# The last product of a transformer block: where sums of activations stand, and how k-tiles are dealt out between quads

## The chip, the cores and the metric

One core of a Trainium2 chip runs the whole kernel. Its engines work side by side: TensorE multiplies matrices (PE in the profile, with its weight loads as PEld), VectorE (DVE) and ScalarE (ACT) do elementwise work, GpSimd (POOL) fills constants and issues a few transfers, and SyncE (SP) issues the transfers of the weights. The metric is the device time of one execution in microseconds, lower is better.

## The reference, cut to what matters

The kernel computes one block with a mixer and a feed-forward part, for 256 tokens and a width of 2048. The change touches the feed-forward part:

```python
h = rms_norm(x, norm_ffn_pre[l])
u = causal_depthwise_conv(h @ w_up[l], ffn_conv_w[l], ffn_conv_b[l])
u_g, u_v = jnp.split(u, 2, axis=-1)
x = x + rms_norm((jax.nn.silu(u_g) * u_v) @ w_down[l], norm_ffn_post[l])
```

`w_up` is 2048 x 11264 and `w_down` is 5632 x 2048, all in float32. The activations `silu(u_g) * u_v` (called a here) have 5632 features, which are 44 k-tiles of 128 features for the last product.

## The kernel before, in words

**Numbers in two parts.** Every float32 operand of a product is split into a high part (a copy to a shorter format, by ACT: `high`) and a low part (the difference, by DVE: `rest`). A product is three matmuls: high by high, high by low and low by high. A tile of weights of 128 x 1024 costs one ACT copy and one DVE subtraction.

**The up projection** (the loop at line 1173). For each of 44 k-tiles i two feature tiles of `w_up` are multiplied on TensorE (`ftile`, lines 151 to 183); DVE and ACT then scale them, apply the convolution of width three, and multiply the gate by the value. The result is split and stored in `gh` and `gl`. The temporary `a` comes from a ring of five buffers with the tag `fa`. The order of this work is left to a planner that simulates the engines and takes what has the highest priority; only some pieces carry a higher priority.

**The last product** (from line 1221). It is computed in two halves of 1024 output columns, `Pair(0)` and `Pair(1)`, each with four result banks (two token halves by two blocks of 512 columns). Of the 44 k-tiles, 28 are *plain* (list `PLAIN`): each costs 4 x 3 = 12 matmuls of 128 x 512. The other 16 are taken two at a time, in 8 pairs (`EARLY + LATE`): a *quad* treats two k-tiles by two token halves by two column blocks as a product of 2 x 2 blocks, and computes it with seven block products in place of eight, as Strassen and Winograd do. A quad so costs 7 x 3 = 21 matmuls instead of 24, but needs sums of weights and sums of activations.

The sums of weights are formed when a quad is prepared (`quad`, line 1267): four DVE additions of 512 columns between four pairs of `high` and `rest`, called b, a, t and 4 in the names of tiles (`whiq_7t` is the high part of t of quad 7).

The sums of activations (`sums`, line 1161) take a0 and a1 of the pair. For the pairs in `EARLY` they are formed in the up projection, as soon as the second k-tile is there, and kept in `se`. For the pairs in `LATE` they are formed in the last product by `late` (line 1329): DVE adds the two parts of both k-tiles back together, then five more DVE operations and two ACT copies follow; the results go to `sl`.

**What sets the order in the last product.** `fixed` (line 975) puts each instruction of DVE behind the one given before it, and the same for ACT, so that the order in the text is the order on these engines. `in_line` does the same for TensorE. The split weights live in a ring of four buffers for the high and four for the low parts (`ring`); a copy into a buffer waits until TensorE has finished with what was there. The raw weights arrive through SP's queue in a ring of five buffers (`fetch`, line 101); a fetch waits until its buffer is free. In the first half the program goes through the quads j = 0 to 7: some plain tiles, then the quad, then, for even j, the sums of `LATE` pair j // 2. The three remaining plain tiles come last. The second half has its own order, which also prepares six plain tiles ahead of time (`kept`).

**Other places that the change touches.** `diag` (line 291) writes a diagonal matrix that a small product spreads over the partitions; it is called for the first norm (names with h) and for the norm ahead of the feed-forward part (names with f). `ones2` is the constant operand of that second product. POOL's own transfers keep their descriptors in a space on chip whose size line 1501 gives.

Of the kernel before, what the change touches and what calls it, by code (L numbers as in the profile page):

```python
# [23 lines left out]
F32 = mybir.dt.float32  # L24
# [7 lines left out]
T = 256  # L32
# [2 lines left out]
NFT = FF // 128  # L35
EPS = 1e-6

EARLY = [(0, 1), (2, 3), (4, 5), (6, 7)]
LATE = [(8, 9), (11, 12), (13, 14), (15, 16)]
PLAIN = [*range(22, 33), 10, *range(17, 22), *range(33, NFT)]  # L40
BA, BB, BC, BG = 2100, 2200, 2200, 2500
PR = 1000
# [13 lines left out]
def block(ctx: ExitStack, tc: tile.TileContext, x, xf, fp, cst, rows, sgw, w1, w2, wf_a, wt_bv, wf_bu, wf_c,  # L56
          wt_vs, wf_q, wt_g, wt_p, wt_o, wf_up, wt_dn, wt_dq, out):
    nc = tc.nc
# [3 lines left out]
    P0 = ctx.enter_context(tc.tile_pool(name="p0", bufs=1))  # L62
# [88 lines left out]
    def ftile(src, mov):  # L151

        hs = granule(src)
        ps = PS.tile([128, 2, T], F32, tag="acc", name=f"ps{uid[0]}")
        mm_f(ps, hs, mov)
        return ps
# [54 lines left out]
    def fsum(ps, dst, scale=1.0, rb=None):  # L211

        t1 = T1["pool"].tile([128, T], F32, tag="q", bufs=T1["bufs"], name=f"t1_{uid[0]}")
        with tc.high_priority(offset=int(PR)):
            S.activation(t1, ps[:, 1], AF.Copy)  # L215
            V.tensor_add(t1 if rb is not None else dst, ps[:, 0], t1)  # L216
            if rb is not None:
                V.scalar_tensor_tensor(dst, t1, scale, rb, op0=ALU.mult, op1=ALU.mult)
# [28 lines left out]
    def q1(name, shape=(128, T)):  # L247
        return P1.tile(list(shape), F32, tag="q", bufs=12, name=name)
# [40 lines left out]
    G.memset(ones, 1.0 / 1024)  # L289

    def diag(r, nm):
        dg = P0.tile([128, 128], F32, tag="dg", bufs=2, name=f"dg{nm}")
        return dg, V.tensor_scalar(dg, ident, r, None, op0=ALU.mult).ins

    def norm1(parts, nm, n=1):

        v = PZ.tile([128, n], F32, tag=f"ssv{n}", bufs=4, name="ssv" + nm)
        V.reduce_sum(v, parts, axis=AX.X)
        variance[0] = V.tensor_scalar(v, v, 1.0 / D, EPS, op0=ALU.mult, op1=ALU.add).ins
        return rsqrt(PZ, v, n, nm)  # L300
# [55 lines left out]
    def rms_sum():  # L356

        ssp = bank([128, 2], "ssp")
        for t in range(2):
            in_line(lambda: PE.matmul(ssp[:, t:t + 1], lhsT=sq[:, 0, t * 128:t * 128 + 128], rhs=ones[:, 0:1],  # L360
                                      start=True, stop=True).ins)
        with tc.high_priority(offset=int(PR)):
            v = PZ.tile([128, 2], F32, tag="ssv2", bufs=4, name="ssvx")
            V.tensor_scalar(v, ssp, 1024.0 / D, EPS, op0=ALU.mult, op1=ALU.add)
            r0 = rsqrt(PZ, v, 2, "x")
            V.tensor_scalar(rh, r0, 0.5, None, op0=ALU.mult)
            return r0, [diag(r0[:, t:t + 1], f"h{t}")[0] for t in range(2)]
# [607 lines left out]
    def fixed(eng, op, *args, **kw):  # L975

        with ExitStack() as order:
            order.enter_context(tc.high_priority())
            for ins in seq.get(eng, ()):
                order.enter_context(tc.issue_after(ins))  # L980
            seq[eng] = [op(*args, **kw).ins]  # L981
# [131 lines left out]
    P2b_ctx = ExitStack()  # L1113
    se = P2.tile([128, 2, len(EARLY), 3, 128], R, name="se")
    gh = [P2.tile([128, 11, T], R, tag="gh", bufs=4, name=f"gh{i}") for i in range(4)]
    gl = [P2.tile([128, 11, T], R, tag="gl", bufs=4, name=f"gl{i}") for i in range(4)]
    P2b = P2b_ctx.enter_context(tc.tile_pool(name="p2b", bufs=1))
    T1["pool"], T1["bufs"] = P2b, 2
    rb2 = P2b.tile([128, T], F32, name="rb2")
    ones2 = P2b.tile([128, 128], F32, name="ones2")  # L1120
    G.memset(ones2, 1.0)
    raw = [fetch(wf_up[2][:, a:a + 1024], 1024) for a in (0, 1024)]
    hs = []
# [5 lines left out]
    with ExitStack() as order:  # L1129
        order.enter_context(tc.high_priority())  # L1130
        for ins in seq[V] + seq[S]:
            order.enter_context(tc.issue_after(ins))
        junk3 = P2b.tile([128, 512], mybir.dt.bfloat16, tag="fa", bufs=5, name="junk3")
        for t in range(2):
            for c in range(4):
                xc = y1[:, t, c * 512:c * 512 + 512]
                if c % 2:
                    V.scalar_tensor_tensor(junk3, xc, 1.0, xc, op0=ALU.mult, op1=ALU.mult,
                                           accum_out=ss2[:, t, c:c + 1])
                else:  # L1140
                    S.activation(junk, xc, AF.Square, accum_out=ss2[:, t, c:c + 1])
        r2 = norm1(ss2, "f", 2)
# [11 lines left out]
    def g2(k, ts):  # L1154

        return gh[k // 11][:, k % 11, ts], gl[k // 11][:, k % 11, ts]
# [4 lines left out]
    def sums(st, a0, a1, k0, dst, do=loose):  # L1161

        h, l = g2(k0, H2)
        do(V, V.tensor_add, st[:, 1], a0[:, H2], a1[:, H2])
        do(V, V.tensor_sub, st[:, 2], st[:, 1], a0[:, H1])
        do(V, V.tensor_sub, st[:, 3], a1[:, H1], st[:, 2])
        do(S, S.activation, dst[0], st[:, 1:4], AF.Copy)
        do(V, V.tensor_sub, st[:, 0], a0[:, H1], a0[:, H2])
        do(S, S.activation, h, st[:, 0], AF.Copy)
        do(V, V.tensor_sub, dst[1], st[:, 1:4], dst[0].bitcast(F32))  # L1170
        do(V, V.tensor_sub, l, st[:, 0], h.bitcast(F32))

    for i in range(NFT):
        acc = []
        for v in range(2):
            f = 2 * i + v
            with tc.issue_after(pe_last[0]):
                pu = pu2[f] if f < 3 else ftile(wf_up[f], h2)
            s = P2b.tile([128, T], F32, tag="fs", bufs=2, name=f"fs{f}")
            fsum(pu, s, rb=rb2)  # L1180
            a = P2b.tile([128, T], F32, tag="fa", bufs=5, name=f"fa{f}")
            w = [fps[:, C_FW + f * 3 + k:C_FW + f * 3 + k + 1] for k in range(3)]
            S.activation(a, s, AF.Identity, bias=fps[:, C_FB + f:C_FB + f + 1], scale=w[2])
            V.scalar_tensor_tensor(a[:, 1:T], s[:, 0:T - 1], w[1], a[:, 1:T], op0=ALU.mult, op1=ALU.add)
            V.scalar_tensor_tensor(a[:, 2:T], s[:, 0:T - 2], w[0], a[:, 2:T], op0=ALU.mult, op1=ALU.add)  # L1185
            acc.append(a)
        S.activation(acc[0], acc[0], AF.Silu)  # L1187
        V.tensor_mul(acc[0], acc[0], acc[1])
        ts = H1 if i in [k for k, _ in EARLY] else slice(0, T)
        h, l = g2(i, ts)  # L1190
        S.activation(h, acc[0][:, ts], AF.Copy)
        V.tensor_sub(l, acc[0][:, ts], h.bitcast(F32))
        for j, (k0, k1) in enumerate(EARLY):
            if i == k0:
                first = acc[0]
            elif i == k1:
                st = P2b.tile([128, 4, 128], F32, tag="st", name=f"st{j}")
                sums(st, first, acc[0], k0, (se[:, 0, j], se[:, 1, j]))
# [8 lines left out]
    gain = fin[:, 4096:5120]  # L1207
    sl = P2c.tile([128, 2, len(LATE), 3, 128], R, name="sl")
    turn = [0]

    def scratch():
        turn[0] ^= 1
        return fin[:, 5120 + 1024 * turn[0]:6144 + 1024 * turn[0]]

    PAIRS = EARLY + LATE
    ss3 = PZ.tile([128, 2, 8], F32, name="ss3")
# [9 lines left out]
    def rest(lo, x, hi):  # L1226
        fixed(V, V.tensor_sub, lo, x, hi.bitcast(F32))
# [11 lines left out]
    class Pair:  # L1239
# [27 lines left out]
        def quad(self, j):  # L1267
# [19 lines left out]
            rest(l4[:, L], b[:, U], h4[:, L])  # L1287
            src, n = (se, j) if j < len(EARLY) else (sl, j - len(EARLY))
            s1, s2, s4 = ((src[:, 0, n, i], src[:, 1, n, i]) for i in range(3))
# [39 lines left out]
    def late(j):  # L1329
        k0, k1 = LATE[j]  # L1330
        tmp = scratch()
        a = tmp[:, 0:512].rearrange("p (k t) -> p k t", k=2)
        gi, gk = divmod(k0, 11)
        fixed(V, V.tensor_add, a, gh[gi][:, gk:gk + 2].bitcast(F32), gl[gi][:, gk:gk + 2].bitcast(F32))
        sums(tmp[:, 512:].rearrange("p (s t) -> p s t", s=4), a[:, 0], a[:, 1], k0, (sl[:, 0, j], sl[:, 1, j]), fixed)

    NP, NQ, KEEP = len(PLAIN), len(PAIRS), 6
# [2 lines left out]
    first, second = Pair(0), None  # L1340
    i = 0
    for j in range(NQ):
        while i < (j + 1) * (NP - 3) // NQ + (j < 2):
            first.plain(i)
            i += 1
        first.quad(j)
        if j % 2 == 0:
            late(j // 2)
    for i in range(i, NP):
        first.plain(i)  # L1350
    first.combine()
# [2 lines left out]
    i = 0  # L1354
# [45 lines left out]
def _layout(inp):  # L1400
# [65 lines left out]
    plain = c(dn[:, PLAIN].transpose(0, 1, 3, 2, 4)).reshape(2, len(PLAIN), 128, 1024)  # L1466
    k0, k1 = [k for k, _ in EARLY + LATE], [k for _, k in EARLY + LATE]
    quads = np.concatenate([dn[:, k1, 1], dn[:, k1, 0], dn[:, k0, 0], dn[:, k0, 1]], axis=3)
# [42 lines left out]
```

## Time and profile before

| | |
|---|---|
| median of 3 runs | 1584.49 us (1583.78 to 1584.77) |
| profiled execution | 1583.9 us, with a span of 1582.2 us in the profile |
| PE busy | 1567.0 us, 99% of the span |
| DVE busy | 1215.6 us, 77% |
| ACT busy | 884.5 us, 56% |
| transfers | 303.75 MB, mean 192 GB/s |

The span is what the profiler records from the first to the last instruction; the time of the execution also has a little around it. Busy time of an engine is time in which an instruction is on it; the busy time of TensorE is modelled, so that the number of matmuls in a stretch says more than its busy share. In a row of the profile, L981 is line 981 of the kernel: all instructions that go through `fixed` carry that line, and are told apart by their tiles. `wraw`, `whi` and `wlo` are raw, high and low weights; `pd0` and `pd1` are the result banks of the two halves; `fin` is one large buffer that holds results and scratch.

### The profile page before, as it was taken

To read this page: it belongs to the slowest core of one execution; us is meant where nothing else is said; L and a number is where in the kernel's file an instruction comes from. 1 tells how busy PE (TensorE), PEld (TensorE's weight loads), DVE (VectorE), ACT (ScalarE), POOL (GpSimd) and SP (SyncE) were. 2 spreads that over 40 slices of the span, in tenths; PEclk is the share of its full clock that TensorE was granted. 3 is DMA by queue.
4 is the path that set the end of the run, shared out by engine and by line. 5 is a ranking of instruction groups with operands and counts; after the bars stand their busy time and mean duration, and the time that the engine had idled before them with its cause. 6 is when DMAs were issued, how large, how long until landed. Compare 5 with 4: busy or idle time off the path is not lost.

```text
span 1582.2 us, 22327 instructions
## 1 busy us (share of the span) xinstructions
PE 1567.0 (99%) x8185; PEld 1329.6 (84%) x8185; DVE 1215.6 (77%) x2082; ACT 884.5 (56%) x1430; POOL 17.8 (1%) x46
## 2 busy tenths in 40 slices
PE   9999999999999999999999999999999999999997
PEld 7888889888888787788888888888888888777886
DVE  7899999857865555465558987777777777888887
ACT  7544454447647675654456655555555555555563
POOL 1000020000000000000000000000000000000000
PEclk9999999999999999999999999999999999999999
DMA  9555556655764444565773665555555566566663
GB/s 370 187 193 180 191 174 212 195 190 186 236 197 157 156 144 156 162 198 188 241 235 117 198 190 190 188 192 189 188 187 188 190 190 202 168 200 207 211 229 106
DMA packets 84863, 303.75 MB, mean 192 GB/s; under 512 B 9744, under 2 KB 10768, under 8 KB 84240
## 3 DMA queue, kind: packets, MB, share of 16 engines
q1 hardware_dynamic: 83664, 298.11, 57.9%
q0 software_dynamic: 944, 4.19, 0.8%
q8 instruction: 64, 1.05, 0.3%
q14 instruction: 47, 0.39, 0.1%
q10 hardware_dynamic: 144, 0.02, 0.0%
HBM read 299.13 MB, written 2.10 MB: 190 GB/s over the span
## 4 chain that ended last, share of the span: by engine, by line
PE 98%; DVE 1%; ACT 0%; DMA 0%; issue 0%; SPq 0%; DVEq 0%; ACTq 0%
PE ps L173 29%; PE ps L180 15%; PE pd1a L1255 6%; PE pd0b L1255 6%; PE pg L194 6%; PE pg L193 6%; PE pg L195 6%; PE py L194 3%; PE py L195 3%; PE py L193 3%; PE po L193 2%; PE po L194 2%; PE po L195 2%; PE pd1b L1255 1%; PE pd0a L1255 1%; PE pv L193 1%
## 5 line engine op out<-in xcount | busy, mean ns | idle before, releaser
L145 DVE TENSOR_TENSOR wlo<-wraw,whi 128x1024 fp32r<-128x1024 f32 x440 | 536.2, 1221 | 171.8 <-ACT whi L144 164.8
L144 ACT ACTIVATE whi<-wraw 128x1024 fp32r<-128x1024 f32 x440 | 461.2, 1053 | 244.1 <-PE pg L195 100.9
L173 PE MATMUL ps<-h2T,whi 128*128 128x512 f32 x1360 | 325.0, 391 | 0.0
L173 PEld LDWEIGHTS ps<-h2T,whi 128*128 128x128 f32 x1360 | 249.8, 188 | 48.2
L180 PEld LDWEIGHTS ps<-h2T,wlo 128*128 128x128 f32 x1360 | 174.5, 191 | 6.7
L180 PE MATMUL ps<-h2T,wlo 128*128 128x256 f32 x1360 | 176.6, 283 | 0.0
L173 PE MATMUL ps<-hT,whi 128*128 128x512 f32 x640 | 157.4, 392 | 0.0
L215 ACT ACTIVATE t<-ps 128x256 f32<-128x256 f32 x125 | 47.6, 382 | 188.4 <-PE ps L173 188.2
L195 PE MATMUL pg<-whi,hT 128*128 128x512 f32 x384 | 150.9, 393 | 0.0
L194 PE MATMUL pg<-wlo,hT 128*128 128x512 f32 x384 | 150.7, 392 | 0.0
L193 PE MATMUL pg<-whi,hT 128*128 128x512 f32 x384 | 147.6, 393 | 0.0
L173 PEld LDWEIGHTS ps<-hT,whi 128*128 128x128 f32 x640 | 116.0, 188 | 21.3
L216 DVE TENSOR_TENSOR t<-ps,t 128x256 f32<-128x256 f32 x125 | 52.9, 424 | 80.3 <-ACT t L215 80.0
L476 DVE SCALAR_TENSOR_TENSOR cv<-hb,fps,cv 128x256 f32<-128x256 f32 x240 | 105.8, 485 | 0.2 <-ACT cv L472 0.2
L180 PEld LDWEIGHTS ps<-hT,wlo 128*128 128x128 f32 x640 | 84.7, 190 | 4.7
L180 PE MATMUL ps<-hT,wlo 128*128 128x256 f32 x640 | 86.8, 283 | 0.0
L194 PEld LDWEIGHTS pg<-wlo,hT 128*128 128x128 f32 x384 | 72.1, 188 | 16.2 <-issue 1.1
L195 PEld LDWEIGHTS pg<-whi,hT 128*128 128x128 f32 x384 | 72.1, 188 | 15.1 <-issue 0.7
L193 PEld LDWEIGHTS pg<-whi,hT 128*128 128x128 f32 x384 | 71.8, 188 | 14.8 <-issue 0.3
L981 DVE TENSOR_TENSOR wlowraw<-wraw,whiwraw 128x1024 fp32r<-128x1024 f32 x52 | 62.1, 1222 | 13.3 <-ACT whiwraw L981 12.3
L981 ACT ACTIVATE whiwraw<-wraw 128x1024 fp32r<-128x1024 f32 x52 | 53.8, 1055 | 16.6 <-PE ps L173 4.3
L1187 ACT ACTIVATE fa<-fa 128x256 f32<-128x256 f32 x44 | 18.3, 416 | 64.3 <-DVE fa L1185 64.3
(891 smaller groups left out, 2458.6 us busy)
## 6 DMA issues: line engine op xcount, KB each, us to landing
wraw<-in_wf_up_dram SPq DMA_DIRECT2D x176, 512.0 KB, 4.3
wraw<-in_wt_g_dram SPq DMA_DIRECT2D x96, 512.0 KB, 4.2
wraw<-in_wt_dn_dram SPq DMA_DIRECT2D x56, 512.0 KB, 4.6
wraw<-in_wt_p_dram SPq DMA_DIRECT2D x48, 512.0 KB, 4.1
wraw<-in_wf_a_dram SPq DMA_DIRECT2D x32, 512.0 KB, 3.9
wraw<-in_wt_o_dram SPq DMA_DIRECT2D x32, 512.0 KB, 4.6
wraw<-in_wt_dq_dram SPq DMA_DIRECT2D x32, 512.0 KB, 3.6
wraw<-in_wf_bu_dram SPq DMA_DIRECT2D x16, 512.0 KB, 4.4
```

The lines of the kernel that those rows point to most:

```text
L144: S.activation(hi[:, :n], raw[:, :n], AF.Copy)
L145: V.tensor_sub(lo[:, :n], raw[:, :n], hi[:, :n].bitcast(F32))
L173: ins = PE.matmul(ps[:, :, ts], lhsT=ws[k // 8][0][:, c:c + 128], rhs=mov[:, k, :, ts], start=(k == 0 and not t), stop=(k == n - 1), skip_ ...
L180: ins = PE.matmul(ps[:, 1, ts], lhsT=ws[k // 8][1][:, c:c + 128], rhs=mov[:, k, 0, ts], start=False, stop=False, skip_group_check=True).ins
L193: PE.matmul(ps, lhsT=xh, rhs=hi, start=first, stop=False)
L194: PE.matmul(ps, lhsT=xh, rhs=lo, start=False, stop=False)
L195: return PE.matmul(ps, lhsT=xl, rhs=hi, start=False, stop=last).ins
L215: S.activation(t1, ps[:, 1], AF.Copy)
L216: V.tensor_add(t1 if rb is not None else dst, ps[:, 0], t1)
L476: V.scalar_tensor_tensor(ca[:, j], hb[:, j, k:k + T], w(j, k), ca[:, j], op0=ALU.mult, op1=ALU.add)
L981: seq[eng] = [op(*args, **kw).ins]
L1255: ins = PE.matmul(bank, lhsT=a[x], rhs=w[y], start=first and j == 0, stop=last and j == 2).ins
```

## The change

The pair (8, 9) moves from `LATE` to `EARLY`, so that its sums of activations are formed in the up projection. The three sets of sums that stay in the last product are formed ahead of quads 1, 2 and 3, behind the plain tiles that stand before these quads, and no longer behind quads 0, 2, 4 and 6. The plain tiles of the first half are dealt out as 5, 4, 4, 4, 2, 2, 2, 2 ahead of the eight quads (before: 4, 3, 2, 3, 3, 3, 3, 4), with three left for the end as before. The order of the second half is as it was. To hold the larger `se`, memory is found elsewhere: the diagonal tiles and `ones2` take buffers of rings that exist already (`q` and `fa`), and the space for POOL's descriptors is halved.

```diff
-EARLY = [(0, 1), (2, 3), (4, 5), (6, 7)]
-LATE = [(8, 9), (11, 12), (13, 14), (15, 16)]
+EARLY = [(0, 1), (2, 3), (4, 5), (6, 7), (8, 9)]
+LATE = [(11, 12), (13, 14), (15, 16)]
...
     def diag(r, nm):
-        dg = P0.tile([128, 128], F32, tag="dg", bufs=2, name=f"dg{nm}")
+        dg = q1(f"dg{nm}", (128, 128)) if nm[0] == "h" else small(f"dg{nm}", (128, 128))
...
-    ones2 = P2b.tile([128, 128], F32, name="ones2")
+
+    def small(name, shape=(128, T), dt=F32):
+        return P2b.tile(list(shape), dt, tag="fa", bufs=5, name=name)
+
+    ones2 = small("ones2", (128, 128))
...
-        junk3 = P2b.tile([128, 512], mybir.dt.bfloat16, tag="fa", bufs=5, name="junk3")
+        junk3 = small("junk3", (128, 512), mybir.dt.bfloat16)
...
-            a = P2b.tile([128, T], F32, tag="fa", bufs=5, name=f"fa{f}")
+            a = small(f"fa{f}")
...
     for j in range(NQ):
-        while i < (j + 1) * (NP - 3) // NQ + (j < 2):
+        while i < (5, 9, 13, 17, 19, 21, 23, 25)[j]:
             first.plain(i)
             i += 1
+        if 1 <= j <= len(LATE):
+            late(j - 1)
         first.quad(j)
-        if j % 2 == 0:
-            late(j // 2)
...
-    nc = bacc.Bacc("TRN2", target_bir_lowering=False, num_devices=1, dynamic_dma_scratch_size=4096)
+    nc = bacc.Bacc("TRN2", target_bir_lowering=False, num_devices=1, dynamic_dma_scratch_size=2048)
```

## The prediction, made before the changed kernel ran

> **What bounds the kernel now.** I read the page first, then the clock and busy time in stretches, then the chain of waits and the order of time of each engine in the last product. The page says that TensorE sets the time:
>
> ```profile
> span 1582.2 us, 22327 instructions
> PE 1567.0 (99%) x8185; PEld 1329.6 (84%) x8185; DVE 1215.6 (77%) x2082; ACT 884.5 (56%) x1430; POOL 17.8 (1%) x46
> ```
>
> So only a place where TensorE runs below its own pace can give time back. The view by stretches (us from:to and length, then busy time and instruction count of PE, PEld, DVE, ACT, POOL, then the granted clock, DMA share, GB/s) finds it. The first two rows are the up projection with and without sums of pairs; the last two are the two column halves of the last product, `Pair(0)` and `Pair(1)`:
>
> ```profile
> 870.35:981.60 111.25, 111.25 (x644) 98.40 (x643) 96.92 (x181) 69.60 (x117) 0.00 (x0) 1.00 0.60 191
> 981.60:1092.90 111.30, 111.30 (x642) 98.35 (x641) 87.89 (x141) 63.81 (x100) 0.00 (x0) 1.00 0.59 190
> 1338.94:1458.90 119.96, 116.70 (x506) 94.44 (x505) 101.35 (x132) 63.16 (x73) 0.00 (x0) 1.00 0.60 193
> 1458.90:1573.16 114.26, 114.24 (x505) 94.25 (x503) 96.70 (x117) 62.77 (x76) 0.00 (x0) 1.00 0.57 189
> ```
>
> Both halves issue 28 x 12 + 8 x 21 = 504 matmuls of 128x512 (the rows count one or two of a neighbour), at the same clock of 1.00. The second takes 114.26 us, 0.2267 us for each; the first takes 119.96. The first half therefore holds 119.96 - 114.26 = 5.70 us in which TensorE waits. That is the whole stake of the change; nothing else in the span is slower than its own pace by more than parts of a us.
>
> TensorE's rows in order of time show where it waits (start, duration, instruction, in brackets the idle time and what ended it):
>
> ```profile
> 1354.36 0.39 PE L1255 MATMUL pd0b<-whiq,gl 128*128 128x512 f32 x1
> 1354.87 0.51 PE L1255 MATMUL pd0b<-whiwraw,gh 128*128 128x512 f32 x1
> 1356.12 0.51 PE L1255 MATMUL pd0b<-wlowraw,gh 128*128 128x512 f32 x1 [0.76 <-DVE wlowraw L981]
> 1356.47 0.40 PE L1255 MATMUL pd0b<-whiwraw,gl 128*128 128x512 f32 x1
> ```
>
> The quad's last matmul starts at 1354.36. At the pace the third matmul after it would start at 1354.36 + 3 x 0.227 = 1355.04; it starts at 1356.47, 1.43 late. The waits of this stage, added up (total us, times, longest), have four of this kind:
>
> ```profile
> PE pd0b L1255 <- DVE wlowraw L981: 3.0, 4, 0.8
> ```
>
> In order of time the four stand behind quads 0, 2, 4 and 6: exactly those after which `late` is called. (The bracket counts only the idle time; each wait also stretches the matmuls beside it, so the starts are the better measure.) 5.70 / 4 = 1.43 agrees with the wait worked out above, so these four are all of it.
>
> What made the weights late is seen on ACT and DVE:
>
> ```profile
> 1350.08 0.63 ACT L981 ACTIVATE whiq<-wraw 128x512 fp32r<-128x512 f32 x1 [1.27 <-PE pd0b L1255]
> 1353.13 0.52 ACT L981 ACTIVATE sl<-fin 128x384 fp32r<-128x384 f32 x1 [2.42 <-DVE fin L981]
> 1353.57 0.30 ACT L981 ACTIVATE gh<-fin 128x128 fp32r<-128x128 f32 x1
> 1353.77 2.94 ACT L981 ACTIVATE whiwraw<-wraw 128x1024 fp32r<-128x1024 f32 x3
> ```
>
> ```profile
> 1351.36 0.68 DVE L981 TENSOR_TENSOR fin<-gh,gl 128x512 f32<-128x512 f32 x1
> 1352.07 1.15 DVE L981 TENSOR_TENSOR fin<-fin 128x128 f32<-128x128 f32 x4
> 1353.69 0.56 DVE L981 TENSOR_TENSOR sl<-fin,sl 128x384 fp32r<-128x384 f32 x1 [0.47 <-ACT sl L981]
> 1354.17 0.28 DVE L981 TENSOR_TENSOR gl<-fin,gh 128x128 fp32r<-128x128 f32 x1
> 1354.85 3.50 DVE L981 TENSOR_TENSOR wlowraw<-wraw,whiwraw 128x1024 fp32r<-128x1024 f32 x3 [0.39 <-ACT whiwraw L981]
> ```
>
> The order on both engines is written out (`fixed`), and the buffers of split weights are a ring of four. The quad's last copy (`whiq`) waits for TensorE to free a buffer and so starts just when TensorE begins the quad. From there to the quad's end are only 21 x 0.227 = 4.76 us, and the sums take 3.49 of them (1351.36 to 1354.85). The next plain tile's copy stands behind the sums in ACT's line.
>
> **The change, part by part.**
>
> *Matmuls.* Same eight pairs, same plain tiles, same 504 matmuls for each half: 0.
>
> *Sums no longer behind a quad: -5.6.* After a quad without sums the next plain tile is in time. Behind quad 3:
>
> ```profile
> 1390.32 1.06 ACT L981 ACTIVATE whiwraw<-wraw 128x1024 fp32r<-128x1024 f32 x1 [0.73 <-PE pd0b L1255]
> 1391.42 3.90 DVE L981 TENSOR_TENSOR wlowraw<-wraw,whiwraw 128x1024 fp32r<-128x1024 f32 x3 [1.10 <-ACT whiwraw L981]
> 1393.70 0.39 PE L1255 MATMUL pd0b<-wlowraw,gh 128*128 128x512 f32 x1
> ```
>
> One third of the 3.90 is 1.30, so the low part is ready at 1392.72 and needed at 1393.70: 0.98 to spare. With the change every quad is followed this way. The first wait alone, four times, is 5.72; the two halves differ by 5.70. I leave 0.1 for small rests and take 5.6; the least that the four starts allow, with the bracket of 0.76 alone, is 3.0.
>
> *Sums in front of quads 1, 2 and 3: 0.* What waits behind them on ACT and DVE is now the preparation of that quad. Four plain tiles stand between the quads there. Quad 7 of the kernel before also has four plain tiles ahead of it, and no sums directly ahead:
>
> ```profile
> 1434.90 3.49 DVE L981 TENSOR_TENSOR wlowraw<-wraw,whiwraw 128x1024 fp32r<-128x1024 f32 x3
> 1439.01 0.69 DVE L981 TENSOR_TENSOR fin<-wraw,wraw 128x512 f32<-128x512 f32 x1 [0.62 <-DMA wraw<-in_wt_dq_dram]
> 1444.45 1.23 DVE L981 TENSOR_TENSOR wloq_7t<-fin,whiq_7t 128x1024 fp32r<-128x1024 f32 x1 [0.54 <-ACT whiq_7t L981]
> 1448.77 0.39 PE L1255 MATMUL pd0a<-wloq_7t,gh 128*128 128x512 f32 x1
> ```
>
> The plain tiles are done on DVE at 1434.90 + 3.49 = 1438.39. Put 3.1 us of sums there (1351.36 to 1354.45) and the quad's first DVE operation moves from 1439.01 to about 1441.5, by 2.5 us. The tightest piece, the low part of `t`, ends at 1445.68 and is needed at 1448.77: 3.1 to spare, of which part was spent waiting for TensorE anyway. Even with all 2.5 taken off, 0.6 are left, and quad 7 itself came behind one of the waits that go. So I take 0. The bounds: no gain (TensorE is at pace there), and at worst the whole 3.49 three times, 10.5.
>
> A rule of the Trainium skill speaks against this step. "TensorE: Matmul & The Clock Gate", in the architectural detail of Part 1, says that ScalarE and VectorE take their instructions strictly in order. By that alone each set of sums still holds up whatever is behind it, and moving three sets gives three holds: with nothing to cover them the sum would end at +10.5 - 5.6, as the second rival has it, against -5.6 by the rows of quad 7. The trace agrees that the lines are in order (the copy at 1353.77 behind the sums), but the lead of the quad's weights over TensorE decides.
>
> *One set fewer in the last product, one more in the up projection.* The pair (8, 9) now costs DVE five 128x128 operations, one of 128x384, less the half of one 128x256:
>
> ```profile
> L1159 DVE TENSOR_TENSOR se<-st,se 128x384 fp32r<-128x384 f32 x4 | 2.2, 552 | 0.0
> L1159 DVE TENSOR_TENSOR st<-fa,fa 128x128 f32<-128x128 f32 x4 | 1.2, 288 | 0.1
> ```
>
> 5 x 0.288 + 0.552 - 0.13 = 1.9 us on DVE over two steps of the loop. The second quoted stretch has 111.30 - 87.89 = 23 us of DVE free, and the first, with four such pairs in it or near it, issues 644 matmuls in 111.25, as full as the second. Cost 0; with that cover gone, 1.9.
>
> *Plain tiles 5, 4, 4, 4, 2, 2, 2, 2 and then 3.* Quads 4 to 7 now have two plain tiles in front of them, where they had three, three, three and four. The kernel has one such spacing, in front of quad 2:
>
> ```profile
> 1374.21 1.22 DVE L981 TENSOR_TENSOR wloq_2t<-fin,whiq_2t 128x1024 fp32r<-128x1024 f32 x1
> 1377.35 0.39 PE L1255 MATMUL pd0a<-wloq_2t,gh 128*128 128x512 f32 x1
> ```
>
> It is ready at 1375.43 and needed at 1377.35, 1.9 to spare. Each quad starts its last copy when TensorE frees a buffer, so each such cycle begins from the same state and the spare does not shrink. A cycle takes TensorE 2 x 2.72 + 4.76 = 10.2 us. SP's queue must bring four tiles of 512 KB, 205 GB/s, in it; the second half brings a further tile behind each of its last five quads (`kept`) and stays at 114.26. Cost 0; if the weights came late, up to about 1 us for each of four quads.
>
> *Buffers.* The diagonal tiles and `ones2` move into rings already there. In the ring of five `fa`, `ones2` and the two diagonals are free after the product that reads them:
>
> ```profile
> L1149 PE MATMUL rbp<-dgf,ones x4: 273/275/275, 875.1 to 875.4; 128*128 128x128 f32 x4
> ```
>
> ```profile
> 878.60 0.59 ACT L1183 ACTIVATE fa<-fs,fps 128x256 f32<-128x256 f32 x1
> ```
>
> That product is over by 875.7; the first `fa` tile takes the one buffer not yet used, and the second, at 878.60 now, is the first to take one of these. Cost 0. The descriptor space of POOL's own transfers is halved, which could make POOL wait longer between its copies of `kd` (16, issued from 214.9 on). Fully one after another at their longest they would take 16 x 5.0 = 80 us, until 295; the first reader is DVE:
>
> ```profile
> L599 DVE TENSOR_SCALAR bt<-kd,fps x32: 257/270/301, 395.5 to 417.5; 128x60 f32<-128x60 f32 x32
> ...
> DMA to landing us min/median/max: 2.0/3.9/5.0
> ```
>
> That is covered by 100 us. The two transfers of `x` (lines 937 and 971) would end, one after the other, by 756.6 + 22 = 779 and are read from 831.6 on:
>
> ```profile
> L971 DVE SCALAR_TENSOR_TENSOR y<-y,rsyo,x x4: 743/746/751, 831.6 to 833.6; 128x512 f32<-128x512 f32 x4
> L937 POOL DMA_DIRECT2D x<-in_x_dram x2: 537/542/548, 756.1 to 756.6; - x2
> ...
> DMA to landing us min/median/max: 7.8/9.4/11.0
> ```
>
> Cost 0.
>
> **The sum.** -5.6 on an execution of 1583.9 us, whose span of 1582.2 has 1.7 us around it: 1578.3. That execution lies 0.6 under the median of 1584.49, so for the median I predict 1578.9.
>
> **Rivals.**
> - *New waits in part of the places.* The margins of 0.6 to 1.9 us come from rows of a neighbouring order, and the loosely ordered up projection may settle another way. Three sums at 0.5 to 1, or 1.9 us in the up projection, or two quads at 1: 1 to 4 us come back, 1580 to 1583.
> - *The sums hold up the quad (slower).* If the quad's preparation has no lead over TensorE, three times 3.49 replaces four times 1.4: 1578.9 + 10.5 = 1589.4. It decides from 2.9 us for each set on: 3 x 2.9 = 5.6 + 3.2. Against it stands the 3.1 us of spare at quad 7; for it, only that the four waits of today are of the same kind.
> - *The waits stay.* If they were the ring's and not the sums', the next plain tile would still be late: 1584.5. Against it: quads 1, 3, 5 and 7 have no sums behind them and no wait.
>
> **How the numbers follow.** What a measurement of this kernel can tell from no change is about 0.2%, 3.2 us. The likeliest case has 0.72, with its own range 1577.9 to 1580. New waits have 0.15, of which about two thirds end faster by over 3.2 us and the rest within. The waits stay: 0.04. The sums hold up the quad: 0.09. That makes faster 0.82, same 0.09, slower 0.09. The range goes from 1577.6 (all 5.70, and a little in the noise of the runs shown, which spread over 1 us) to 1583.0, which takes in the new waits.
>
> **What would show it.** In the profile after: the first half at 114.3 us; no idle time of TensorE that ends with the low part of a plain tile; ACT's sums (`sl`) at three places, each ahead of a quad's first copy and with the plain tile's copies in front; quads 1 to 3 without a wait of TensorE; the stretches of the up projection as full as before, with one more set of `se`. I am wrong if TensorE's idle time reappears in front of quads 1, 2 and 3, in the run of quads 4 to 7 behind a DMA, or near 876 us behind `fa`.

## The result, and the profile after

The changed kernel takes 1578.96 us (median; 1578.74 to 1580.11), the kernel before 1584.09 us beside it (1583.67 to 1584.77). The ratio is 0.9969, with an interval of 0.9957 to 0.998: faster by 5.1 us, 0.3%.

The page of the profiled execution, and its stretches (us from:to and length, then busy time and instructions of PE, PEld, DVE, ACT, POOL, then granted clock, DMA share, GB/s):

```profile
span 1578.4 us, 22322 instructions
PE 1565.2 (99%) x8185; PEld 1330.2 (84%) x8185; DVE 1214.5 (77%) x2081; ACT 885.4 (56%) x1430; POOL 17.7 (1%) x46
```

```profile
870.35:981.60 111.25, 111.25 (x643) 98.47 (x642) 98.78 (x187) 70.42 (x119) 0.00 (x0) 1.00 0.60 191
981.60:1092.90 111.30, 111.30 (x642) 98.39 (x641) 87.64 (x141) 63.40 (x99) 0.00 (x0) 1.00 0.60 189
1338.62:1453.04 114.42, 114.42 (x506) 94.82 (x505) 98.70 (x125) 63.58 (x71) 0.00 (x0) 1.00 0.63 202
1453.04:1568.70 115.66, 114.98 (x504) 94.06 (x503) 96.63 (x117) 62.55 (x76) 0.00 (x0) 1.00 0.56 187
```

The up projection is as full as before with the added set of sums in the first stretch (98.78 us of DVE instead of 96.92). The first half of the last product has become as short as the second half was. In the chain of waits (start, us, what) it is TensorE alone:

```profile
1338.80 14.96 PE pd0b L1259 x66
1353.76 2.72 PE pd0a L1259 x12
1356.48 12.92 PE pd0b L1259 x57
1369.40 2.72 PE pd0a L1259 x12
...
1444.20 8.84 PE pd0b L1259 x39
1453.04 7.03 PE pd1a L1259 x31
```

From here on "first half" means the time from the first piece of `pd0b` in this chain to the first of `pd1a`: 1453.04 - 1338.80 = 114.24 us, and 1458.90 - 1339.10 = 119.80 by the same measure before. So the profile shows -5.56 there.

The span shrank by 3.8 only. The rest is accounted for: the stage starts 0.30 earlier, the second half takes 115.84 where it took 114.25 (+1.59), and the end behind TensorE's last matmul is 0.47 longer (9.52 us in place of 9.05). -5.56 - 0.30 + 1.59 + 0.47 = -3.80. This execution, at 1580.11 us, is the slowest of the seven; in the median less is given back. The section on pair_only returns to the 0.47.

What the second half gives back is one wait of TensorE behind quad 6. The chain leads to it through DVE and the fetches of a quad's weights:

```profile
1511.86 1.24 DVE kept L981
1513.11 5.42 DMA wraw<-in_wt_dq_dram
...
1525.27 1.23 DVE kept L981
1526.51 6.55 DMA wraw<-in_wt_dq_dram
...
1540.92 1.23 DVE wlowraw L981
1542.16 0.04 issue
1542.20 6.89 PE pd1a L1259 x29
```

How the sums now lie in front of quad 1: the timelines of ACT, DVE and TensorE of the changed kernel (start in us, us, what, and in brackets the idle time before it and what ended it):

```profile
1361.59 0.53 ACT L981 ACTIVATE sl<-fin 128x384 fp32r<-128x384 f32 x1 [3.06 <-DVE fin L981]
...
1362.22 1.05 ACT L981 ACTIVATE whiq_1b<-wraw 128x1024 fp32r<-128x1024 f32 x1
...
1369.48 1.06 ACT L981 ACTIVATE whiwraw<-wraw 128x1024 fp32r<-128x1024 f32 x1 [0.73 <-PE pd0b L1259]
```

```profile
1354.94 5.03 DVE L981 TENSOR_TENSOR wlowraw<-wraw,whiwraw 128x1024 fp32r<-128x1024 f32 x4 [1.09 <-ACT whiwraw L981]
1359.89 0.69 DVE L981 TENSOR_TENSOR fin<-gh,gl 128x512 f32<-128x512 f32 x1
...
1362.82 0.69 DVE L981 TENSOR_TENSOR fin<-wraw,wraw 128x512 f32<-128x512 f32 x1
...
1367.63 1.22 DVE L981 TENSOR_TENSOR wloq_1t<-fin,whiq_1t 128x1024 fp32r<-128x1024 f32 x1
```

```profile
1367.88 0.39 PE L1259 MATMUL pd0b<-whiq_1b,se 128*128 128x512 f32 x1
...
1370.82 0.39 PE L1259 MATMUL pd0a<-wloq_1t,gh 128*128 128x512 f32 x1
```

The sums (the addition at 1359.89 and six more operations, not five as in the description of `late`) take DVE from 1359.89 to 1362.82, 2.9 us, while TensorE works on the four plain tiles. The low part of t is ready at 1368.85 and needed at 1370.82: 1.97 to spare. Behind the quad the plain tile's copy at 1369.48 waits only for TensorE.

### The profile page after: what moved, and what is told of

Read it like the earlier page. It is cut to its first block, busy times and chain, and to the rows that moved or that the text cites. A ratio compares the mean times of both kernels' runs of the same rounds, so it can differ in the third digit from the quotient of the medians.

```text
span 1578.4 us, 22322 instructions
## 1 busy us (share of the span) xinstructions
PE 1565.2 (99%) x8185; PEld 1330.2 (84%) x8185; DVE 1214.5 (77%) x2081; ACT 885.4 (56%) x1430; POOL 17.7 (1%) x46
## 4 chain that ended last, share of the span: by engine, by line
PE 97%; DVE 1%; DMA 1%; ACT 0%; issue 0%; SPq 0%; DVEq 0%; ACTq 0%
PE ps L173 29%; PE ps L180 15%; PE pd0b L1259 6%; PE pg L194 6%; PE pg L193 6%; PE pg L195 6%; PE pd1a L1259 5%; PE py L194 3%; PE py L195 3%; PE py L193 3%; PE po L195 2%; PE po L194 2%; PE po L193 2%; PE pd0a L1259 1%; PE pv L193 1%; PE pd1b L1259 1%
```

## The experiments

The question is whether the gain comes from the place of the sums and the lead that they have there, as predicted, or from one of the other parts: the dealing of the plain tiles, or the set of sums that left the last product. Five runs do one part alone or undo one; three lengthen the sums; the rest go after the wait in the second half. Each is timed beside the kernel before on its chip (1584.1 to 1584.4 us).

| run | time, us | ratio (interval) | first half, us | second half, us |
|---|---|---|---|---|
| before | 1584.09 | | 119.80 | 114.25 |
| changed | 1578.96 | 0.9969 (0.9957 to 0.998) | 114.24 | 115.84 |
| order_only | 1579.93 | 0.997 (0.9958 to 0.9981) | 115.81 | 115.05 |
| plains_only | 1583.93 | 0.9997 (0.9988 to 1.0006) | 119.76 | 115.00 |
| late_behind | 1583.65 | 0.9995 (0.9986 to 1.0004) | 118.38 | 114.87 |
| plains_before | 1580.80 | 0.9975 (0.9966 to 0.9984) | 115.76 | 115.25 |
| pair_only | 1583.80 | 0.9995 (0.9986 to 1.0004) | 118.42 | 115.54 |
| sums_x3 | 1578.85 | 0.9968 (0.9956 to 0.998) | 114.24 | 117.04 |
| sums_x4 | 1580.91 | 0.9979 (0.997 to 0.9988) | 115.90 | 115.89 |
| sums_x9 | 1594.59 | 1.0067 (1.0053 to 1.0081) | 129.40 | 116.65 |

The two halves come from the one profiled execution of each run, read as above; the second half ends with TensorE's last matmul in the chain.

### Only the place of the sums: order_only

```diff
-        first.quad(j)
-        if j % 2 == 0:
-            late(j // 2)
+        if 1 <= j <= len(LATE):
+            late(j - 1)
+        first.quad(j)
```

> The kernel before with one edit: each of its four sets of sums stands in front of quads 1 to 4 instead of behind quads 0, 2, 4 and 6; plain tiles 4, 3, 2, 3, 3, 3, 3, 4 and the pair (8, 9) in LATE as before. Theory (place and lead): the four waits of 1.43 us behind the quads go. In front of a quad with four plain tiles the profile after has 1.97 us to spare (low part of t of quad 1 ready at 1368.85, needed 2.95 us after the quad's start at 1367.87, so at 1370.82); each plain tile fewer takes 2.72 us of lead and 1.13 us of VectorE work away, so 0.4 us to spare with three and 1.2 us too late with two. Quad 2 has two: first half 114.3 + 1.2 = 115.5 us, time about 1579.6. Rival (the sums hold up whatever stands behind them): four new waits of up to 3.5 us, first half 120 to 128 us, time 1584 or more.

The first half is 115.81 us, 0.3 from the forecast. The four waits behind the quads are gone, and one place is left where TensorE stands idle, in front of quad 2, which has two plain tiles ahead of it:

```profile
1373.83 0.50 PE L1255 MATMUL pd0b<-wloq_2b,se 128*128 128x512 f32 x1 [0.45 <-DVE wloq_2b L981]
```

So the place alone brings 4.0 of the 5.56 us. The forecast had the low part of t as the piece that comes late; the first idle time is already at that of b.

### Only the dealing: plains_only

```diff
-        while i < (j + 1) * (NP - 3) // NQ + (j < 2):
+        while i < (5, 9, 13, 17, 19, 21, 23, 25)[j]:
```

> The kernel before with the plain tiles dealt out as 5, 4, 4, 4, 2, 2, 2, 2 and nothing else: sums behind quads 0, 2, 4 and 6, pair (8, 9) in LATE. Theory (place and lead): the four waits stay, since the lead behind a quad is the quad's own 4.76 us whatever stands in front: first half 119.9 us, time 1584. Rival (the dealing makes the gain): first half near 114 us, time near 1579.

119.76 us, and the same four waits (us in total, times, longest):

```profile
PE pd0b L1255 <- DVE wlowraw L981: 3.0, 4, 0.8
```

The dealing by itself is worth nothing.

### The place undone: late_behind

```diff
-        if 1 <= j <= len(LATE):
-            late(j - 1)
         first.quad(j)
+        if j < len(LATE):
+            late(j)
```

> The changed kernel with its three sets of sums directly behind quads 0, 1 and 2 instead of in front of quads 1, 2 and 3; all else as changed. Theory (place and lead): three waits of 1.43 us come back behind quads 0, 1 and 2: first half 114.4 + 4.3 = 118.7 us, time about 1583.3. Rival (dealing or the set fewer made the gain, not the place): first half 114.4 us, time 1579.

118.38 us: three sets behind three quads, three waits, (118.38 - 114.24) / 3 = 1.38 each. Four plain tiles in front of each of these quads do not help, since the sums stand behind them.

```profile
PE pd0b L1259 <- DVE wlowraw L981: 2.3, 3, 0.8
```

### The dealing undone: plains_before

```diff
-        while i < (5, 9, 13, 17, 19, 21, 23, 25)[j]:
+        while i < (j + 1) * (NP - 3) // NQ + (j < 2):
```

> The changed kernel with the plain tiles dealt out as before (4, 3, 2, 3, 3, 3, 3, 4); sums in front of quads 1, 2 and 3. Theory (place and lead): quads 1 and 3 have three plain tiles in front and 0.4 us to spare, quad 2 has two and is 1.2 us late: first half 114.4 + 1.2 = 115.6 us, time about 1580.2. Rival (the dealing is worth nothing): first half 114.4 us, time 1579.

115.76 us, 1.52 more than the changed kernel, at the same place as in order_only (0.43 idle in front of quad 2). The dealing is worth 1.5 us once the sums stand in front: it puts the plain tiles where the sums need cover.

### Only the pair and the buffers: pair_only

```diff
-        while i < (5, 9, 13, 17, 19, 21, 23, 25)[j]:
+        while i < (j + 1) * (NP - 3) // NQ + (j < 2):
...
-        if 1 <= j <= len(LATE):
-            late(j - 1)
         first.quad(j)
+        if j % 2 == 0 and j < 5:
+            late(j // 2)
```

> The changed kernel with the place of the sums and the dealing of plain tiles as before: the pair (8, 9) summed in the up projection, the moved buffers, the halved descriptor space, and three sets of sums behind quads 0, 2 and 4. Theory (place and lead): one wait of 1.43 us fewer, the up projection and the buffers cost nothing: first half 114.3 + 4.3 = 118.6 us, time about 1582.7. Rival (the added set costs TensorE time in the up projection): its stretch from 870 us on issues fewer than 642 matmuls in 111.25 us, and up to 1.9 us come back, time about 1584.5.

118.42 us, one wait of 1.38 fewer than before. The up projection with the added set:

```profile
870.35:981.60 111.25, 111.25 (x643) 98.42 (x642) 98.77 (x187) 70.41 (x119) 0.00 (x0) 1.00 0.60 192
```

643 matmuls in 111.25 us, against 644 and 642 in the two stretches before: the added set costs nothing there. The median is only 0.56 under the kernel before; in the profile the second half takes 1.29 of the 1.38 back. Both the buffers and the halved descriptor space are in this run, and show no cost in the stages that they touch.

They do not come free all the same. The end of the kernel, from TensorE's last matmul in the chain to the end of the span, takes 9.05 us before, 8.99 in order_only and 8.95 in plains_only. In pair_only it takes 9.52, and in every other profile with the pair and the buffers 9.46 to 9.52 (kept_five apart, whose chain leaves TensorE earlier). The added half microsecond lies behind the issue of the last output transfer: the span ends 3.0 us after it before (issue at 1579.2), and 3.5 us after it in the changed kernel (1574.9). So this part of the change costs about 0.5 us. Whether the pair, the buffers or the descriptor space does it, and how, no run separates.

### How much room the sums have: sums_x4, sums_x9, sums_x3

```diff
-        fixed(V, V.tensor_add, a, gh[gi][:, gk:gk + 2].bitcast(F32), gl[gi][:, gk:gk + 2].bitcast(F32))
+        for _ in range(4):
+            fixed(V, V.tensor_add, a, gh[gi][:, gk:gk + 2].bitcast(F32), gl[gi][:, gk:gk + 2].bitcast(F32))
```

This is sums_x4; the other two have `range(9)` and `range(3)`.

> The changed kernel with the first VectorE addition of each set of sums in the last product done four times instead of once (same result): three times 0.61 = 1.83 us longer. Theory (place and lead): that is within the 1.97 us that the low part of t has to spare in front of quads 1 to 3: first half 114.4 to 114.7 us, time as changed, about 1579. Rival (what stands in front of a quad is not covered): three waits of 1.8 us, first half 119.9 us, time about 1584.5.

> The changed kernel with that addition done nine times: 8 x 0.61 = 4.88 us longer for each of the three sets. Theory (place and lead): 4.88 - 1.97 = 2.9 us of wait in front of each of quads 1, 2 and 3: first half 114.4 + 8.7 = 123.1 us, time about 1587.7, slower than the kernel before. Rival (the lead is larger than counted, by buffers further back): less than half of that, time under 1583.

Both forecasts were too low: 115.90 and 129.40 us, +1.66 and +15.16 where 0 to 0.3 and 8.7 were expected. One part is the length of an addition that rewrites its own result: the group of four takes 2.86 us and one alone 0.69, so each is 0.72 and not 0.61. The other is the rule that I used. DVE's first operation for quads 1, 2 and 3 with four additions, and with nine (there with a wait of DVE between quads 2 and 3):

```profile
1365.22 0.68 DVE L981 TENSOR_TENSOR fin<-wraw,wraw 128x512 f32<-128x512 f32 x1
...
1381.50 0.69 DVE L981 TENSOR_TENSOR fin<-wraw,wraw 128x512 f32<-128x512 f32 x1
...
1397.77 0.69 DVE L981 TENSOR_TENSOR fin<-wraw,wraw 128x512 f32<-128x512 f32 x1
```

```profile
1369.01 0.68 DVE L981 TENSOR_TENSOR fin<-wraw,wraw 128x512 f32<-128x512 f32 x1
...
1388.91 0.68 DVE L981 TENSOR_TENSOR fin<-wraw,wraw 128x512 f32<-128x512 f32 x1
...
1397.75 1.23 DVE L981 TENSOR_TENSOR wlowraw<-wraw,whiwraw 128x1024 fp32r<-128x1024 f32 x1 [1.01 <-ACT whiwraw L981]
...
1410.45 0.69 DVE L981 TENSOR_TENSOR fin<-wraw,wraw 128x512 f32<-128x512 f32 x1
```

A cycle of quad, four plain tiles and sums takes TensorE 4.76 + 4 x 2.72 = 15.64 us. With four additions DVE needs 16.28 (1381.50 - 1365.22), with nine 19.90. Less the 2.17 and 5.81 that were added, both leave 14.1: DVE has 1.5 us free in a cycle. Once the copies no longer wait for TensorE, DVE sets the pace, and every cycle loses what goes beyond 1.5. The spare of 1.97 is there once; it is not there anew for every quad. TensorE's rows with four additions bear this out: counted from the start of the half, it begins quad 1 in time, and quads 2, 3 and 4 begin 0.40, 1.02 and 1.66 us later than in the changed kernel, so the last two cycles lose 0.62 and 0.64, where 2.17 - 1.54 = 0.63.

With nine additions the rule gives only a lower bound. It leaves 5.81 - 1.54 = 4.27 for each cycle, 12.8 for three, and the half grew by 15.16. The cycle from quad 2 to quad 3 took 21.54 us (1410.45 - 1388.91) in place of 19.90. Of these 1.64 us, 1.46 are waits of DVE for ACT's copies of plain tiles (the 1.01 above, and 0.45 behind it). What held up those copies is not followed here.

The next run was chosen by the rule of the free time:

> The first addition of each set of sums done three times. With it done four times the work of VectorE for one cycle of four plain tiles, sums and quad was 16.28 us (quad 2's first operation at 1381.58, quad 3's at 1397.86) against TensorE's 15.64; the extra is 2.18, so without it 14.10. Theory now (VectorE's free time in a cycle, 15.64 - 14.10 = 1.54 us, decides, not a spare of 1.97 that every quad has anew): two additions more are 1.45 us, just within it: first half 114.2 to 114.6 us, time as changed. Rival (each addition in front costs some): a third of what four cost beyond one for each addition, first half 115.3 us.

114.24 us, the changed kernel's to the hundredth, and quads 1 and 2 begin on DVE 15.64 apart:

```profile
1363.80 0.69 DVE L981 TENSOR_TENSOR fin<-wraw,wraw 128x512 f32<-128x512 f32 x1
...
1379.44 0.69 DVE L981 TENSOR_TENSOR fin<-wraw,wraw 128x512 f32<-128x512 f32 x1
```

The median agrees (1578.85, with 1579.43 for the changed kernel on the same chip). This run does not tell the two rules apart, since the added 1.45 us lie below the spare of 1.97 as well as below 1.54; the 0.62 and 0.64 of sums_x4 do. It rules out that every addition in front costs something, for which 115.3 was forecast.

### The wait in the second half: second_dealt, kept_five, and the changed kernel again

```diff
-        while i < 3 + -((3 + KEEP - NP) * j // (NQ - 1)):
+        while i < (3, 5, 8, 11, 14, 17, 20, 22)[j]:
```

> The changed kernel with one plain tile of the second half moved from in front of quad 1 to in front of quad 4: 3, 2, 3, 3, 3, 3, 3, 2 instead of 3, 3, 3, 3, 2, 3, 3, 2. The profile after has one wait of 1.4 us in the second half, behind quad 6, at the end of a chain of kept tile, fetch of a quad's weights (5.4 and 6.6 us) and the quad's VectorE work, which turns more slowly than TensorE's 12.9 us for a cycle. Theory (that chain starts late at quad 4, where five fetches meet a cycle of 10.2 us): with 12.9 us there the chain keeps its lead, the wait goes, second half 114.3 us, time 1577.6 to 1578.8. Rival (the wait is an accident of single fetches): it comes in some executions whatever the dealing, time 1579 as changed; or quad 1 becomes late with two plain tiles, time 1580.

1578.66 us (ratio 0.9967, 0.9954 to 0.9979), and the second half at 114.25 without a wait. That is what the theory wanted, but 0.3 us beside a spread of 1 us is no verdict. So it went to one chip with the changed kernel:

> The changed kernel unchanged, beside the two variants of its second half and on the same chip: 1579 us, first half 114.2 us; a wait behind quad 6 of the second half in the profile of 0 to 1.6 us (theory: it is there in most executions, since the chain that makes it is there whatever the single fetches take; rival: an accident, seen in a minority).

> The second half dealt out as 3, 2, 3, 3, 3, 3, 3, 2, once more, on the chip of the changed kernel. Theory (the chain of kept tile, fetch and quad starts with more lead): no wait in the second half, 114.25 us, and 0.5 to 1.2 us under the changed kernel. Rival (accident): the same time as the changed kernel.

1579.43 for the changed kernel (ratio 0.9971, 0.996 to 0.9983) and 1579.41 for the other dealing (0.9969, 0.9957 to 0.9981): no difference. The changed kernel's second half is 115.22, and this time the other dealing's is 115.26. The chain of that execution shows why more lead did not last (DVE's `kept`, fetch, DVE's first operation for the next quad):

```profile
1511.29 1.23 DVE kept L981
1512.53 5.51 DMA wraw<-in_wt_dq_dram
1518.13 0.70 DVE fin L981
...
1524.76 1.23 DVE kept L981
1526.01 5.16 DMA wraw<-in_wt_dq_dram
1531.27 0.70 DVE fin L981
```

The chain goes round in 1531.27 - 1518.13 = 13.1 us, and 13.5 the time before, against TensorE's 12.9 for three plain tiles and a quad. It closes on itself: a quad's second weight tile is fetched into the buffer that the kept tile frees, the kept tile stands behind the previous quad's work on DVE, and that work waits for its fetch. Without its fetch of 5.2 us the round of 13.1 leaves 8.0 for the rest, so of the 5.0 to 6.6 us for a fetch about 5 is what a cycle of 12.9 can bear (an estimate). In the profile before, where the second half has no wait, the fetches at the places of 5.42 and 6.55 took 5.4 and 4.7 us.

```diff
-    NP, NQ, KEEP = len(PLAIN), len(PAIRS), 6
+    NP, NQ, KEEP = len(PLAIN), len(PAIRS), 5
```

> The changed kernel with five tiles kept for the end of the second half in place of six, the sixth put back among the plain tiles (3, 3, 3, 3, 3, 3, 3, 2 and five kept). Theory (the chain): quad 4 has 12.9 us in front of it, so no wait in the second half, as with the other dealing: 114.25 us, 0.5 to 1.2 us under the changed kernel. Against it: the last blocks of the end are 3.4 us instead of 4.1 us long, and if the work on the results needs the longer ones the tail grows by up to 0.7 us.

1580.14 us (0.9972, 0.9962 to 0.9982), 0.7 above the changed kernel on that chip. The theory failed here too: counted by TensorE's starts, the second half still loses 1.3 us by its end. The objection in the forecast holds in part: behind TensorE's last matmul, at 1568.44, the span of 1578.4 has 9.9 us left, 0.4 more than in the changed kernel. The chain leaves TensorE before the last block and ends on DVE, which is still busy with earlier results:

```profile
1554.16 10.90 PE pd1a L1259 x48
1565.08 0.69 DVE fin L1163
1565.77 2.65 DVE fin L1400 x4
```

No run gave a version that is measurably faster than the changed kernel.

## Why the prediction was right

**Sums no longer behind a quad, -5.6: right.** The first half fell by 5.56 us. That it is the place which does it is shown from both sides: order_only takes the four waits away with nothing else changed, late_behind brings three of them back at 1.38 each. The rival "the waits stay" falls with this.

**Sums in front of quads 1, 2 and 3, 0: right, for a narrower reason than given.** TensorE waits at none of them. I read the room from quad 7 of the kernel before, as a lead of the quad's weights: 0.6 at least and 3.1 at most. The changed kernel has 1.97, and sums_x4 and sums_x9 show that this lead is spent once, while DVE's free 1.5 us in each cycle decide whether it comes back. The rival "the sums hold up the quad" is what sums_x9 shows: TensorE waits there in front of each of quads 1 to 3, and the kernel is slower than the one before (1.0067). With 2.17 us added to each set (sums_x4) it is still faster (0.9979), so the turn lies between 2.17 and 5.81 us more for each set. The rule of the Trainium skill that was weighed there ("TensorE: Matmul & The Clock Gate", architectural detail of Part 1) has ScalarE and VectorE work strictly in order. The trace of sums_x9 agrees: DVE's first operation for quad 1 comes at 1369.01, behind the lengthened sums, where the changed kernel has it at 1362.82.

**The pair in the up projection, 0: right.** 643 matmuls in 111.25 us.

**The dealing, 0: right as a cost; as a gain I had not counted it.** The prediction asked only what two plain tiles ahead of quads 4 to 7 would cost. With the sums in front, the old dealing leaves quad 2 short and costs 1.5 us (plains_before). Quads 4 to 7 run without a wait of TensorE, as read from quad 2 before.

**The buffers, 0: right in the stages that the prediction looked at, not at the end of the kernel.** With the pair, the buffers and the halved descriptor space together, the end behind TensorE's last matmul is about 0.5 us longer (9.46 to 9.52 in place of 8.95 to 9.05). The sum has no term for it.

**The sum.** For the median 1578.9 was forecast and 1578.96 measured. The agreement to 0.1 is luck, since two things cancel: the base of the forecast, 1584.49, lies 0.4 above the 1584.09 that the kernel before took beside the changed one, and the gain is 5.13 where 5.6 was forecast. The added 0.5 us at the end would account for that gap by itself: -5.56 + 0.47 = -5.09. What the second half does to the median is open. The forecast took it as untouched, from an execution in which it had no wait at all (114.25); in the profiles of all other kernels with the same order of the second half it took 114.87 to 117.04. Two of these, order_only and plains_only, have neither the pair nor the buffers, so the wait does not need them. How often the kernel before has it is not known, since only one execution of it was profiled; so it is not shown whether the change makes it longer.

## What to carry to other kernels

Work that must stand somewhere in a fixed order belongs where the consumer still has several tiles ready, not where the ring of buffers has just run dry: the same 3 us cost 1.4 us behind a quad and nothing behind four plain tiles. How much can be put there is decided by two numbers, the lead at that place and the free time of the engine in one full cycle, and here only the second was renewed. When a gain in one stage arrives short in the whole, compare every stretch of the span over all kernels that share a part of the change, the end included. Before a stretch of a profile is taken as "at its own pace", look for a chain in it that closes on itself, as fetch, DVE and buffer do here, and compare its time round with the cycle.

## What was not expected of the hardware

A fetch of 512 KB took 5.0 to 6.6 us in the chains of the second half, which single out the slow ones. The median from issue to landing for quad weights over the whole run was 3.6 us before and 3.9 in the changed kernel. The core moved 219 GB/s in the changed kernel between 1504 and 1550 us.

A DVE addition of 128x512 that overwrites the result of the one before it starts 0.72 us behind it. Where the next operation touches nothing of the one before, it started after 0.61 (1365.94 to 1366.55 in sums_x4). What makes the difference was not tested.
